# A causal mask, a key transpose and a sum of squares moved between TensorE and VectorE in a fused decoder layer

## The chip, the cores and the metric

The kernel runs on one core of one Trainium2 chip. The metric is the device time of one execution in microseconds; lower is better. The engines named below are TensorE (PE, matmuls and transposes through an identity), PEld (its weight loads), VectorE (DVE), ScalarE (ACT), GpSimd (POOL) and the DMA queues. PSUM is the memory that TensorE writes to, in banks of 128 partitions by 512 fp32 columns.

## The reference

One decoder layer over 256 tokens of width 2048, all fp32: a half-weighted SwiGLU block, a mixing layer, and another half-weighted SwiGLU block. The mixing layer has a sparse-attention branch and an mLSTM branch, each projected, gated and summed. What the change touches:

```python
def rms_norm(x, gain):
    x32 = x.astype(jnp.float32)
    y = x32 * lax.rsqrt(jnp.mean(x32 * x32, axis=-1, keepdims=True) + EPS)
    return (y * gain.astype(jnp.float32)).astype(x.dtype)

def masked_softmax(s, mask):
    s = jnp.where(mask, s.astype(jnp.float32), NEG_INF)
    return jax.nn.softmax(s, axis=-1) * mask
...
    # nsa_attention: 16 query heads in 4 groups, head width 64
    q = rms_norm(q, q_gain) * (d ** -0.5)
    p_cmp = masked_softmax(jnp.einsum("bgrsd,bgcd->bgrsc", q, kc), cmp_mask)
    kb = rms_norm(k_slc, ks_gain)      # keys of the selected blocks
    kw = rms_norm(k_win, kw_gain)      # keys of the window
    ps = masked_softmax(ss, smask)     # q against the selected keys, causal
    pw = masked_softmax(jnp.einsum("bgrqd,bgkd->bgrqk", qi, kwi), wmask)   # window, causal
    return gt[..., 0:1] * o_cmp + gt[..., 1:2] * o_slc + gt[..., 2:3] * o_win
```

With 256 tokens every block is selected and the window covers everything, so both the selected and the window attention are plain causal attention with keys and values of their own.

## The kernel before, in words

**Weights.** Every projection streams its weight from HBM in tiles of 128x1024 fp32 (512 KB). ScalarE rounds a tile to a high part (whi) and VectorE subtracts it to get a low part (wlo, split_lo); TensorE multiplies high and low parts with high and low parts of the activations, in matmuls of 512 or 256 columns that accumulate in the banks named mm. A unit is one block of output columns. Each tile is processed in two halves (e = 0 and 1) of six matmuls of 512 columns or their equivalent.

**Side work.** Everything else (norms, attention, mLSTM) is written as Python generators called jobs, which alternate: one part that issues TensorE work into a side bank (names sc and tr, two banks each), a yield, one part for the other engines, a yield. After each half tile, step() may let one job issue its TensorE part between the weight matmuls; uptake() issues the other part. All of this happens when the program is built: the order of the instructions on each engine is fixed, and Estimate keeps a running count of each engine's time from simple costs of shape and engine. A job is taken only under this rule in step(), with LAG = 4.0 and MARGIN = 0.3:

```python
if max(est.q["V"], est.q["A"]) > now + LAG or max(free["sc"][0], free["tr"][0]) > now:
    return None
j = next((j for j in jobs if ready(j) + MARGIN <= now and j is not cur.get("late")), None)
```

Jobs whose name begins with ca or R have their matmuls spread among the next weight matmuls, two or three at a time (mul). drain() issues all jobs that are left, one after another, with no weight matmuls between them.

**Norms.** residual() accumulates the squares of 16 blocks of the transposed activations in acc (128 x 2 x 256, even blocks in one half and odd ones in the other). The job g_r then sums over partitions with matmuls against a matrix of ones, which are fp32 and run in two passes each, computes 1/sqrt on VectorE and spreads it over a row (RB). It runs three times, as R0, R1 and R2.

**Attention.** normed() normalises queries and keys per head. g_kk(g) transposes the keys of group g, for both kinds of keys, and writes high and low parts (kk) into both partition halves. g_nsa() goes through 32 items: 4 groups, two halves t of the queries (the second has 256 keys, the first 128) and 4 heads. Step n transposes the probabilities of item n-3 and issues the scores of item n (both kinds of keys in one bank) and, as a third matmul, the mask: an identity in bf16 times the mask maskb, added in the bank. Then exps() takes the maximum on VectorE and exponentials on ScalarE, and scale() scales the item before on VectorE. After each four items pv() multiplies with the values. Between groups the job waits for g_ca (attention over compressed keys) and g_kk of the next group. After a step it yields the time at which the work of the item before last is done.

**Order around it.** The attention runs beside the units mv and mo of the mLSTM's projections. The next unit begins with mlstm_open(), which calls drain() before it can give the attention's memory to the mLSTM. In the profile this drain lies between 988.9 and 1007.8 us. g_mlstm has two mask matmuls per head of its own, which the change leaves alone.

Of the kernel before, what the change touches and what calls it, by code (L numbers as in the profile page):

```python
# [18 lines left out]
S = 256  # L19
# [95 lines left out]
def layer(ctx: ExitStack, tc: tile.TileContext, xt, cols, w_small, b_in,  # L115
# [282 lines left out]

    def g_r():

        ps = psS()
        for t in range(2):
            for a in range(2):
                T.matmul(ps[:, 2 * t:2 * t + 2], acc[:, a, t * 128:t * 128 + 128], ones[:, 0:2], start=a == 0, stop=a == 1)
        yield
        R = small(2, tag="R", bufs=2)
        rsqrt(R, ps[:, 0:4].rearrange("p (t e) -> p t e", e=2)[:, :, 0], 2, 1.0 / D)
        for t in range(2):
            V.tensor_scalar(dg[:, t, :], ident, R[:, t:t + 1], None, op0=OP.mult)
        cur["R"] = R  # L410
        yield
        ps = psS()
        for t in range(2):
            T.matmul(ps[:, t * 128:t * 128 + 128], ones, dg[:, t, :], start=True, stop=True)
        yield
        A.copy(RB, ps[:, :S])
        yield
# [134 lines left out]
    def mixing():  # L552
# [31 lines left out]
        def start():  # L584
            close1()
            openp("O")
            openp("V", "right")
            openp("N")
            O, N = env["O"], env["N"]
            env["O_"] = O.tile([128, 8, 2, S], F32R, name="O_")  # L590
            env["brow"] = O.tile([128, 384], F32R, name="brow")
            env["gat"] = O.tile([128, 2, 48], F32, name="gat")
            env["negM"] = O.tile([128, 2, 4], F32, name="negM")
            env["em"] = O.tile([128, 2, 4], F32, name="em")
            env["kn"] = N.tile([128, 2, 2, S], F32, name="kn")
            env["v"] = N.tile([128, 2, 2, S], F32, name="v")
            env["kc"] = N.tile([128, 4, 2, 32], F32R, name="kc")
            env["vcz"] = N.tile([128, 4, 4, 64], F32, name="vcz")
            nc.sync.dma_start(w2k, cw2k.rearrange("(k p) n -> p k n", p=128))
            nc.sync.dma_start(w2v, cw2v.rearrange("(k p) n -> p k n", p=128))  # L600
            G.memset(env["brow"].bitcast(F32), 0.0)
            G.memset(env["kc"].bitcast(F32), 0.0)
# [146 lines left out]
        def normed(src, dst, n):  # L749

            yield
            sq = t4() if n == 16 else t2()
            A.activation(sq, src, AF.Square)
            yield
            yield
            ss = small(n, tag="ss", bufs=2)
            V.tensor_reduce(ss, sq.rearrange("p t (h d) -> p (t h) d", d=64), AX, OP.add)
            yield
            yield
            rs = small(n, tag="rs", bufs=2)  # L760
            rsqrt(rs, ss, n, 1.0 / 64)
            yield
            yield
            V.tensor_mul(dst.rearrange("p t (h d) -> p (t h) d", d=64),
                         src.rearrange("p t (h d) -> p (t h) d", d=64),
                         rs[:, :, None].to_broadcast([128, n, 64]))
            yield

        def q_done(c):
# [13 lines left out]
            return f  # L783

        def g_qn(q, c):
            yield from normed(q, q, 16)
            if c == 0:
                env["qg"] = env["N"].tile([128, 1], F32, name="qg")
                V.tensor_scalar(env["qg"], col(C_QG), 0.125, None, op0=OP.mult)
# [19 lines left out]
        def g_kk(g):  # L809

            kk = env["k", g] = env["N"].tile([128, 2, 2, S], F32R, name=nm("kk"), tag="kk", bufs=2)
            tr = psT()[0:64].rearrange("p (i s) -> p i s", i=2)
            for i in range(2):
                for t in range(2):
                    T.transpose(tr[:, i, t * 128:t * 128 + 128], env["kn"][:, i, t, g * 64:g * 64 + 64], ident)
            yield
            each = [(i, cl[0:64, cg:cg + 1], slice(o, o + 64)) for i, cg in enumerate((C_KSG, C_KWG)) for o in (0, 64)]
            for i, gain, o in each:
                A.activation(kk[o, 0, i, :], tr[:, i, :], AF.Identity, scale=gain)
            for i, gain, o in each:  # L820
                V.scalar_tensor_tensor(kk[o, 1, i, :], tr[:, i, :], gain, kk[o, 0, i, :].bitcast(F32),
                                       op0=OP.mult, op1=OP.subtract)
            yield

# [6 lines left out]
            return f  # L831

        def g_k(k, i):
            yield from normed(k, env["kn"][:, i], 8)


        def gates_of(g):
# [37 lines left out]
        def g_nsa():  # L875
# [3 lines left out]
            def scores(g, t, r):  # L879
                n = 128 * (t + 1)  # L880
                ps = psS().rearrange("p (b s) -> p b s", b=2)
                for i in range(2):
                    T.matmul(ps[:, :, 0:n], env["q", g][:, r, t * 128:t * 128 + 128], env["k", g][:, i, :, 0:n],
                             start=i == 0, stop=False)
                T.matmul(ps[:, :, n - 128:n], identb, maskb[:, None, :].to_broadcast([128, 2, 128]),
                         start=False, stop=True)
                return ps

            def exps(g, t, r, ps):
                n = 128 * (t + 1)  # L890
                nx, sm = small(2, tag="nx", bufs=6), small(2, tag="nx", bufs=6)
                V.tensor_reduce(nx, ps[:, :, 0:n], AX, OP.max, negate=True)
                p = t2(n)
                for b in range(2):
# [524 lines left out]
```

## Time and profile before

| | |
|---|---|
| median of 3 runs | 2196.39 us (2196.3 to 2196.83) |
| the profiled execution | 2196.61 us |
| span of its instructions | 2194.9 us, 28308 instructions |
| TensorE busy | 2182.7 us (99%), 10865 matmuls |
| VectorE busy | 1429.3 us (65%) |
| ScalarE busy | 1043.8 us (48%) |
| DMA | 414 MB, 189 GB/s mean |

The span goes from the first to the last instruction in the profile; 1.7 us of the execution lie outside it. All instructions carry line 110, that of the helper which records each operation, so groups are told apart by engine, operation and tile names (out<-in). Tile names are cut to their letters: t is any of several scratch tiles, nx a maximum, sc and tr the side banks.

### The profile page before, as it was taken

Reading aid. Unit: us, or ns where it says so; the run is one execution under the profiler, and the core shown is the slowest. Engines: PE = TensorE matmul, PEld = TensorE weight load, DVE = VectorE, ACT = ScalarE, POOL = GpSimd, SP = SyncE. Lnnn points to the kernel's source line nnn. Section 1 sums busy time; section 2 is a strip of 40 time slices with the busy share of each in tenths; the row PEclk is TensorE's granted clock in tenths of the full one; section 3 lists DMA queues with packets and bytes.
Section 4 is the critical chain, followed back from the end, with each engine's and each line's share of the span. In section 5 each row is a group of like instructions: output and inputs, shape, how many; then the busy total and the mean of one; then the engine's idle time right before and its main releaser. Section 6 shows DMA issues by size and latency. Waiting matters only on the chain.

```text
span 2194.9 us, 28308 instructions
## 1 busy us (share of the span) xinstructions
PE 2182.7 (99%) x10865; PEld 1833.8 (84%) x10865; DVE 1429.3 (65%) x1895; ACT 1043.8 (48%) x1302; POOL 32.1 (1%) x62
## 2 busy tenths in 40 slices
PE   9999999999999999999999999999999999999999
PEld 7888888888888888777888888888888888888888
DVE  6766676666555678876777666666667666765554
ACT  6444444444444465666764444555444444443432
POOL 0000000000000000001100000000000000000000
PEclk9999999999999999999999999999999999999999
DMA  7666666666665676544556666566666666666664
GB/s 251 185 204 195 192 182 202 195 189 196 189 188 179 196 238 185 163 132 118 163 168 206 199 205 200 174 201 185 199 186 196 195 199 184 198 195 200 196 199 125
DMA packets 281047, 414.45 MB, mean 189 GB/s; under 512 B 13456, under 2 KB 146704, under 8 KB 280912
## 3 DMA queue, kind: packets, MB, share of 16 engines
q1 hardware_dynamic: 279408, 408.08, 61.2%
q0 software_dynamic: 1360, 4.46, 0.8%
q8 instruction: 85, 1.39, 0.3%
q14 instruction: 50, 0.41, 0.1%
q10 hardware_dynamic: 144, 0.11, 0.0%
HBM read 410.50 MB, written 2.10 MB: 188 GB/s over the span
## 4 chain that ended last, share of the span: by engine, by line
PE 97%; DVE 1%; DMA 0%; ACT 0%; issue 0%; SPq 0%; DVEq 0%; ACTq 0%
PE mm L110 94%; PE tr L110 2%; PE sc L110 2%; DVE wlo L110 0%; DMA raw<-in_wu_dram 0%; DMA raw<-in_w_in_dram 0%; DVE nx L110 0%; DVE t L110 0%; DVE y L110 0%; ACT t L110 0%; ACT whi L110 0%; ACT kk L110 0%; DVE mo L110 0%; DVE rt L110 0%; DVE kk L110 0%
## 5 line engine op out<-in xcount | busy, mean ns | idle before, releaser
L110 DVE TENSOR_TENSOR wlo<-raw,whi 128x1024 fp32r<-128x1024 f32 (+1 forms) x771 | 936.6, 1226 | 617.2 <-ACT whi L110 613.5
L110 PE MATMUL mm<-whi,XX 128*128 128x512 f32 x3904 | 1222.1, 391 | 4.9 <-ACT whi L110 4.9
L110 ACT CAST whi<-raw 128x1024 fp32r<-128x1024 f32 (+1 forms) x771 | 804.1, 1050 | 885.8 <-PE mm L110 843.5
L110 PEld LDWEIGHTS mm<-whi,XX 128*128 128x128 f32 x3904 | 734.3, 188 | 156.5 <-ACT whi L110 4.9
L110 PE MATMUL mm<-wlo,XX 128*128 128x512 f32 x1952 | 762.8, 391 | 0.5 <-DVE wlo L110 0.5
L110 PE MATMUL mm<-H,whi 128*128 128x512 f32 (+1 forms) x1496 | 446.4, 382 | 0.5 <-DVE y L110 0.5
L110 PEld LDWEIGHTS mm<-wlo,XX 128*128 128x128 f32 x1952 | 367.2, 188 | 75.6 <-DVE wlo L110 2.0
L110 PEld LDWEIGHTS mm<-H,wlo 128*128 128x128 f32 x1408 | 264.8, 188 | 58.6
L110 PE MATMUL mm<-H,wlo 128*128 128x256 f32 x1408 | 284.2, 278 | 0.0
L110 PEld LDWEIGHTS mm<-H,whi 128*128 128x128 f32 x1496 | 228.5, 189 | 0.9 <-DVE y L110 0.7
L110 DVE STREAM_TRANSPOSE ht<-sh 32x256 f32<-32x256 f32 x352 | 153.5, 436 | 6.4
L110 PE MATMUL mm<-XX,whi 128*128 128x512 f32 x272 | 87.7, 401 | 0.0
L110 PE MATMUL mm<-M__9899,whi 128*128 128x512 f32 x256 | 80.0, 394 | 0.0
L110 PEld LDWEIGHTS mm<-XX,wlo 128*128 128x128 f32 x272 | 51.0, 188 | 12.0 <-DVE wlo L110 0.7
L110 PEld LDWEIGHTS mm<-M__9899,wlo 128*128 128x128 f32 x256 | 48.1, 188 | 10.9
L110 PE MATMUL mm<-XX,wlo 128*128 128x256 f32 x272 | 55.0, 279 | 0.2 <-DVE wlo L110 0.2
L110 PE MATMUL mm<-M__9899,wlo 128*128 128x256 f32 x256 | 50.5, 279 | 0.0
L110 PEld LDWEIGHTS mm<-XX,whi 128*128 128x128 f32 x272 | 42.3, 189 | 1.0 <-issue 0.2
L110 ACT ACTIVATE sg<-mm,R 128x512 f32<-128x512 f32 x40 | 25.4, 686 | 33.0 <-PE mm L110 31.6
L110 PE MATMUL mm<-whi,h__8408 128*128 128x512 f32 x128 | 40.2, 390 | 0.0
L110 PE MATMUL mm<-whi,O__5735 128*128 128x512 f32 x128 | 40.1, 389 | 0.0
L110 PEld LDWEIGHTS mm<-M__9899,whi 128*128 128x128 f32 x256 | 38.6, 188 | 0.1
(192 smaller groups left out, 969.0 us busy)
## 6 DMA issues: line engine op xcount, KB each, us to landing
raw<-in_wu_dram SPq DMA_DIRECT2D x176, 512.0 KB, 3.9
raw<-in_wd_dram SPq DMA_DIRECT2D x176, 512.0 KB, 4.7
raw<-in_wg_dram SPq DMA_DIRECT2D x175, 512.0 KB, 4.4
raw<-in_w_in_dram SPq DMA_DIRECT2D x168, 512.0 KB, 3.8
raw<-in_w_out_dram SPq DMA_DIRECT2D x32, 512.0 KB, 4.7
raw<-in_wb_n_dram SPq DMA_DIRECT2D x16, 512.0 KB, 4.7
raw<-in_wb_m_dram SPq DMA_DIRECT2D x16, 512.0 KB, 4.0
bias<-in_b_in_dram POOLq DMA_DIRECT2D x17, 256.0 KB, 4.0
```

The source lines that it names most:

```text
L110: return g(out, *a, **k)
```

## The change

Three edits. The mask matmul of the attention's scores is gone; instead VectorE adds the mask to the last 128 columns of both halves of the bank, in place, before it takes the maximum. The normalised keys are stored with the two kinds side by side for each group (kn becomes token half, group, kind, width), so that one transpose of 128 columns holds both kinds, one kind in each partition half, and g_kk issues two transposes, not four. In g_r VectorE first adds the two halves of acc, in a step of its own, and the sum over partitions takes two matmuls, not four.

```diff
     def g_r():
 
+        yield
+        V.tensor_add(acc[:, 0], acc[:, 0], acc[:, 1])
+        yield
         ps = psS()
         for t in range(2):
-            for a in range(2):
-                T.matmul(ps[:, 2 * t:2 * t + 2], acc[:, a, t * 128:t * 128 + 128], ones[:, 0:2], start=a == 0, stop=a == 1)
+            T.matmul(ps[:, 2 * t:2 * t + 2], acc[:, 0, t * 128:t * 128 + 128], ones[:, 0:2], start=True, stop=True)
...
-            env["kn"] = N.tile([128, 2, 2, S], F32, name="kn")
+            env["kn"] = N.tile([128, 2, 4, 2, 64], F32, name="kn")
...
-            V.tensor_mul(dst.rearrange("p t (h d) -> p (t h) d", d=64),
-                         src.rearrange("p t (h d) -> p (t h) d", d=64),
-                         rs[:, :, None].to_broadcast([128, n, 64]))
+            V.tensor_mul(dst, src.rearrange("p t (h d) -> p t h d", d=64),
+                         rs.rearrange("p (t h) -> p t h", t=2)[:, :, :, None].to_broadcast([128, 2, n // 2, 64]))
...
-            yield from normed(q, q, 16)
+            yield from normed(q, q.rearrange("p t (h d) -> p t h d", d=64), 16)
...
-            tr = psT()[0:64].rearrange("p (i s) -> p i s", i=2)
-            for i in range(2):
-                for t in range(2):
-                    T.transpose(tr[:, i, t * 128:t * 128 + 128], env["kn"][:, i, t, g * 64:g * 64 + 64], ident)
+            tr = psT()[:, 0:S]
+            for t in range(2):
+                T.transpose(tr[:, t * 128:t * 128 + 128], env["kn"][:, t, g].rearrange("p i d -> p (i d)"), ident)
             yield
-            each = [(i, cl[0:64, cg:cg + 1], slice(o, o + 64)) for i, cg in enumerate((C_KSG, C_KWG)) for o in (0, 64)]
-            for i, gain, o in each:
-                A.activation(kk[o, 0, i, :], tr[:, i, :], AF.Identity, scale=gain)
-            for i, gain, o in each:
-                V.scalar_tensor_tensor(kk[o, 1, i, :], tr[:, i, :], gain, kk[o, 0, i, :].bitcast(F32),
+            each = [(i, slice(64 * i, 64 * i + 64), cg, slice(o, o + 64)) for i, cg in enumerate((C_KSG, C_KWG)) for o in (0, 64)]
+            for i, s, cg, o in each:
+                A.activation(kk[o, 0, i, :], tr[s], AF.Identity, scale=cl[s, cg:cg + 1])
+            for i, s, cg, o in each:
+                V.scalar_tensor_tensor(kk[o, 1, i, :], tr[s], cl[s, cg:cg + 1], kk[o, 0, i, :].bitcast(F32),
                                        op0=OP.mult, op1=OP.subtract)
...
-            yield from normed(k, env["kn"][:, i], 8)
+            yield from normed(k, env["kn"][:, :, :, i, :], 8)
...
                     T.matmul(ps[:, :, 0:n], env["q", g][:, r, t * 128:t * 128 + 128], env["k", g][:, i, :, 0:n],
-                             start=i == 0, stop=False)
-                T.matmul(ps[:, :, n - 128:n], identb, maskb[:, None, :].to_broadcast([128, 2, 128]),
-                         start=False, stop=True)
+                             start=i == 0, stop=i == 1)
                 return ps
...
                 nx, sm = small(2, tag="nx", bufs=6), small(2, tag="nx", bufs=6)
+                own = ps[:, :, n - 128:n]
+                V.tensor_add(own, own, maskb[:, None, :].to_broadcast([128, 2, 128]))
                 V.tensor_reduce(nx, ps[:, :, 0:n], AX, OP.max, negate=True)
```

## Rows read from the trace of the kernel before

**Rows 1.** The profile's page: busy time of each engine with its share of the span and its instructions, and the chain that ended last, by engine.

```profile
PE 2182.7 (99%) x10865; PEld 1833.8 (84%) x10865; DVE 1429.3 (65%) x1895; ACT 1043.8 (48%) x1302; POOL 32.1 (1%) x62
...
PE 97%; DVE 1%; DMA 0%; ACT 0%; issue 0%; SPq 0%; DVEq 0%; ACTq 0%
```

**Rows 2.** Groups of matmuls by shape over the whole span: the costliest one and the three that the change edits. The columns are the shape, how many, busy us and mean ns of one, and the idle time before them.

```profile
L110 PE MATMUL mm<-whi,XX 128*128 128x512 f32 x3904 | 1222.1, 391 | 4.9 <-ACT whi L110 4.9
...
L110 PE MATMUL sc<-maskb,identb 128*128 128x256 bf16 x32 | 9.1, 283 | 0.0
...
L110 PE MATMUL sc<-ones,acc 128*128 128x2 f32 x24 | 3.0, 230 | 0.0
...
L110 PE MATMUL tr<-ident,kn 128*64 128x128 f32 x16 | 2.4, 272 | 0.0
```

**Rows 3.** The timeline of TensorE in five short stretches: start, length from the first start to the modelled last end, and how many matmuls of one kind. Left-out lines inside a stretch are weight matmuls (mm, 512 columns), one unless said: one at 848.09; one at 882.14; one at 889.38; one at 49.82 and two from 50.50; in the last stretch, which is one item, two transposes of 128 columns at 904.85, two scores of 512 at 904.99, the mask at 905.54 and one weight matmul at 905.58.

```profile
48.99 0.62 PE L110 MATMUL mm<-whi,XX 128*128 128x512 f32 x2
49.45 0.50 PE L110 MATMUL sc<-ones,acc 128*128 128x2 f32 x4
...
50.13 0.50 PE L110 MATMUL sc<-ones,acc 128*128 128x2 f32 x4
...
51.04 0.40 PE L110 MATMUL mm<-wlo,XX 128*128 128x512 f32 x1
...
847.50 0.40 PE L110 MATMUL mm<-whi,XX 128*128 128x512 f32 x1
847.73 0.60 PE L110 MATMUL tr<-ident,kn 128*64 128x128 f32 x4
...
848.40 0.39 PE L110 MATMUL mm<-wlo,XX 128*128 128x512 f32 x1
...
881.54 0.63 PE L110 MATMUL mm<-whi,XX 128*128 128x512 f32 x2
882.00 0.38 PE L110 MATMUL tr<-ident,t 128*128 128x128 f32 x2
...
882.45 0.63 PE L110 MATMUL mm<-whi,XX 128*128 128x512 f32 x2
...
888.86 0.40 PE L110 MATMUL mm<-whi,XX 128*128 128x512 f32 x1
889.09 0.40 PE L110 MATMUL sc<-kk,qs 128*128 128x256 f32 x2
889.34 0.28 PE L110 MATMUL sc<-maskb,identb 128*128 128x256 bf16 x1
...
889.69 0.39 PE L110 MATMUL mm<-wlo,XX 128*128 128x512 f32 x1
...
904.61 0.40 PE L110 MATMUL mm<-whi,XX 128*128 128x512 f32 x1
...
905.90 0.39 PE L110 MATMUL mm<-wlo,XX 128*128 128x512 f32 x1
```

**Rows 4.** Windows: the stretch in us and its length, then busy time (and instructions) of PE, PEld, DVE, ACT and POOL, the granted TensorE clock (1.00 is full), the DMA share and GB/s. First the 25 us before the attention, all of the attention among weight matmuls, and the drain; then three stretches in which items of 256 keys run, and as the second of the four one with items of 128 keys.

```profile
864.00:889.00 25.00, 24.24 (x120) 19.88 (x119) 22.55 (x45) 14.53 (x18) 0.54 (x1) 1.00 0.65 190
889.00:988.90 99.90, 99.90 (x561) 77.78 (x559) 79.19 (x163) 61.99 (x170) 1.08 (x2) 1.00 0.49 142
988.90:1007.80 18.90, 17.15 (x127) 11.76 (x125) 13.09 (x40) 13.17 (x53) 0.00 (x0) 1.00 0.11 29
...
898.10:910.90 12.80, 12.80 (x66) 9.79 (x66) 11.26 (x24) 9.54 (x30) 0.00 (x0) 1.00 0.57 165
917.50:932.30 14.80, 14.80 (x96) 11.80 (x95) 11.88 (x26) 8.24 (x27) 0.54 (x1) 1.00 0.56 162
932.30:945.70 13.40, 13.40 (x68) 10.26 (x67) 11.56 (x28) 8.36 (x24) 0.00 (x0) 1.00 0.44 127
...
969.20:985.00 15.80, 15.80 (x82) 12.40 (x81) 12.38 (x27) 8.98 (x23) 0.00 (x0) 1.00 0.40 106
```

**Rows 5.** The timeline of VectorE in the drain, where items of 256 keys run; the bracket at the end of a line is idle time before it and what ended it.

```profile
996.37 0.42 DVE L110 TENSOR_TENSOR O__5735<-tr,O__5735 128x256 fp32r<-128x256 f32 x1 [1.37 <-ACT O__5735 L110]
...
998.22 0.68 DVE L110 TENSOR_REDUCE nx<-sc 128x2 f32<-128x512 f32 x1
998.82 0.15 DVE L110 RECIPROCAL nx<-nx 128x2 f32<-128x2 f32 x1
999.01 0.73 DVE L110 TENSOR_SCALAR t<-t,nx,gat 128x256 f32<-128x256 f32 x2
999.67 0.69 DVE L110 TENSOR_REDUCE nx<-sc 128x2 f32<-128x512 f32 x1
...
1001.12 0.68 DVE L110 TENSOR_REDUCE nx<-sc 128x2 f32<-128x512 f32 x1
```

**Rows 6.** Groups of VectorE instructions by shape over the whole span, columns as in the second group of rows: the queries' low parts, an mLSTM product with three operands, and the add of the compressed scores' mask.

```profile
L110 DVE SCALAR_TENSOR_TENSOR qs<-tr,qg,qs 64x512 fp32r<-64x512 f32 x8 | 6.0, 750 | 4.9 <-ACT qs L110 4.8
...
L110 DVE SCALAR_TENSOR_TENSOR h<-tr,rc,mo 128x256 f32<-128x256 f32 x8 | 3.5, 480 | 0.1
...
L110 DVE TENSOR_TENSOR t<-sc,mcb 128x256 f32<-128x256 f32 x4 | 1.7, 423 | 2.1 <-PE sc L110 2.1
```

**Rows 7.** The instructions on the tile R, the norm's factors: the gates that are scaled by it from PSUM (how many, duration least, median and most in ns, then first and last start in us).

```profile
L110 ACT ACTIVATE sg<-mm,R x40: 682/686/691, 79.6 to 1923.2; 128x512 f32<-128x512 f32 x40
```

**Rows 8.** Who waited for whom, all of the span: TensorE's weight matmuls for the low parts of weights (us in total, times, longest).

```profile
PE mm L110 <- DVE wlo L110: 0.7, 3, 0.3
```

## The prediction

> **What bounds the kernel now.** I read the totals first, then single shapes, then stages. In the totals [rows 1] TensorE is busy 99% of the span and the chain that ended last runs over it for 97%; VectorE is at 65%. Shape by shape [rows 2] nearly all of that is the streamed weights, matmuls of 512 columns; the reader is to see how small the edited shapes are beside them. Their starts [rows 3] lie 0.23 us apart when one follows another: that pitch, not the 0.39 us that a single one lasts, is what a removed matmul is worth. So a TensorE instruction taken out between weight matmuls shortens the run by its pitch.
>
> That holds only where weights stream. The windows by stage [rows 4] show two other places. In the 99.9 us of attention VectorE is already busy 79.2 us, and in the best-filled stretches about 88% of the time. And from 988.9 to 1007.8 the kernel drains: the last unit of VectorE-fed projections is over, mlstm_open calls drain(), and no weight matmul stands between the attention steps. All eight items of the last group lie there. VectorE's rows in the drain [rows 5] are the ones to look at longest: its maxima of the second half begin at 998.22, 999.67 and 1001.12, 1.45 us apart, and the four VectorE pieces in each stretch (maximum, reciprocal, two scalings) follow each other without a gap. There VectorE sets the pace. TensorE's busy row claims 17.15 of 18.9 us for this drain, its weight loads only 11.76.
>
> [...] By the matmul row TensorE would bound the drain, its 0.12 us per mask would count there in full, and the adds would be worth minus 1.0 instead of the plus 2.7 below; by the weight-load row the drain is VectorE's. The gapless 1.45 us decide for the second.
>
> **The parts, on TensorE.** Mask: between the weight matmuls that begin at 888.86 and 889.69 lie two plain pitches (0.46) and three matmuls of 256 columns, two scores and a mask [rows 3]: 0.83 - 0.46 = 0.37, so 0.12 us a mask. There are 32 in attention (the eight of 128 columns belong to the mLSTM and stay) [rows 2]: 3.8 us, of which 24 among weights now, 2.9.
>
> Keys: four transposes of 64 columns cost 847.50 to 848.40 less two pitches, 0.44; two of 128 columns cost 881.54 to 882.45 less three pitches, 0.22 [rows 3]. Four groups, 0.88 us.
>
> Squares: each of three norms issues two runs of four (two fp32 passes per matmul) [rows 2, 3]. From 48.99 to 51.04 are five pitches (1.15) and both runs: 0.90, one run 0.45. With two matmuls kept, not four, one run is left: 3 x 0.45 = 1.35 us.
>
> **On VectorE.** 32 adds of 128x256 with one operand in PSUM. The nearest row is the same add for the compressed scores, also with a bf16 mask, 423 ns [rows 6]; that one writes to SBUF, and no row has VectorE writing to PSUM. Lower bound 0.33, the pitch of two such scalings when nothing depends on the first [rows 5]; upper 0.48, a three-operand pass over 256 elements [rows 6]. I take 0.42, as the shape is the same: 13.4 us in all. The three adds of halves (two operands of 128x256 again, so 0.42) are hidden: the norm's factors have many half tiles before a unit's end wants them (the first sums run at 49.45, the first gate is scaled from PSUM at 79.6 [rows 3, 7]), and the additional step costs about one half tile, 1.4 us. Should that cover be gone it costs 3 x 1.8. The other layout of kn changes strides only, same shapes and counts; gains on partitions 64 to 127 into 0 to 63 are what qs does already (750 ns for twice the columns) [rows 6]. Nothing here issues a DMA or moves one past a queue: the weight tiles keep their places.
>
> The add waits for the score as the maximum did. Behind it on VectorE stand the maximum, the scaling of the item before and the next weight split (wlo). The exponential waits for the first, the transposes for the second, weight matmuls for the third. That wait is short now: 0.7 us in all [rows 8].
>
> **Drain as it stands.** Eight adds. The fourth falls into the 1.37 us that VectorE idles before 996.37 [rows 5]; seven are on the pace: 7 x 0.42 = 2.9, less 0.2 for scores that come earlier without a mask at the two places where VectorE has just waited: plus 2.7. Bounds: 7 x 0.33 less eight masks (1.0), plus 1.3; 8 x 0.48, plus 3.8.
>
> **What slips into it.** This is where I chose. In the stretches in which items of 256 keys run, VectorE is busy 11.26 of 12.8, 11.56 of 13.4 and 12.38 of 15.8 us [rows 4]. Each gets four adds, 1.7 us, and loses four masks, 0.5 us of TensorE: 12.96 in 12.3, 13.26 in 12.9, 14.1 in 15.3. The first two are over-full. The planner in the code doesn't let VectorE fall far behind: no job when its count for VectorE is over 4.0 ahead, nor before the banks of the item before last are free. So it skips half tiles, and the splits go on taking VectorE. If 0.89 is the best fill (11.26/12.8, 22.55/25 [rows 4]), the three need 14.6, 14.9 and 15.8 us, 2.3 + 2.0 + 0.5 more; the half-group of 128 keys at 917.5 (11.88 + 1.7 = 13.6, by 0.89 15.3, against 14.3) 1.0 more. That is 5.8 us, four half tiles of 1.4. A group alternates items with other steps, so about three items are not issued in time, and the compressed attention of the last group, which ends just before the drain now, has its last two steps in it as well.
>
> An item in the drain costs VectorE 1.45 + 0.42 = 1.87. The work that TensorE takes along is worth 904.61 to 905.90 less two pitches and a mask [rows 3]: 1.29 - 0.46 - 0.12 = 0.71. Net 1.16; three, 3.5 us. The compressed steps: a sum, two products of 256 elements at 0.33 and some small ones, 1.35, with the wait for the exponential about 1.7.
>
> **Sum.** 21 masks among weights -2.5, keys -0.88, squares -1.35, drain +2.7, three items +3.5, compressed steps +1.7: +3.2 us. On the profiled execution (2196.61: span 2194.9 and 1.7 around it) that is 2199.8; the median of the runs is 0.2 lower, so 2199.6.
>
> **The rivals.** (1) Nothing slips: VectorE has 20.7 idle us in attention against 24 x 0.42 = 10.1. For it: the total fits, and the third stretch has room. Against: the idle time lies around the p-v steps and group changes, where no item may start. Then -2.9 - 0.88 - 1.35 + 2.7 = -2.4: 2194.0, with the drain's bounds 2192.6 to 2195.1.
> (2) Five to seven items slip and the compressed attention comes late whole (2.5): -2.2 - 0.88 - 1.35 + 2.7 + 5.8 to 8.1 + 2.5, plus 6.6 to 8.9: 2203.0 to 2205.3. It decides when the first group loses three half tiles or more, since the later ones start from its backlog. For it: VectorE at 22.55 of 25 us before attention begins; against: the p-v steps in which it catches up.
> (3) The change is worth all it removes: the new order leaves no more exposed in the drain than today's, 3.8 + 0.88 + 1.35 = 6.0: 2190.4. The gapless pieces of the drain speak against it.
> (4) TensorE's clock falls in the longer, sparser drain. [...]
>
> **How the numbers follow.** Forecast (two to four items slip, 2198.2 to 2201.2 with the bounds of the add) 0.54; (1) 0.18; (2) 0.19; (3) 0.05; (4) 0.04. The range 2193.0 to 2204.5 leaves out (3), the low end of (1) and the top of (2). A measurement here tells 0.2%, 4.4 us, from no change: 2192.0 and 2200.8. Faster: (3) and a little of (1), 0.07. Slower: (2), (4) and the upper part of the forecast, 0.38. Same: 0.55.
>
> **What would show it.** In the profile after: no maskb matmul in attention; eight kn transposes, twelve ones matmuls; a VectorE add on sc near 0.42 us, 32 times; VectorE over 85% in attention; more than eight score pairs in the drain, with maxima near 1.9 us apart; a drain some 8 us longer and an attention stage shorter. Wrong if the drain still begins with the last group, if it begins deeper than four items before it, if weight matmuls wait for wlo, or if the clock leaves 1.00.

## The result, and the profile after

| | before | after |
|---|---|---|
| median of 4 runs side by side | 2196.46 us (2196.3 to 2196.83) | 2212.9 us (2212.35 to 2213.21) |
| ratio, 95% interval | | 1.0075, 1.0063 to 1.0088 |
| the profiled execution and its span | 2196.61, 2194.9 us | 2212.35, 2210.0 us |

The change costs 16.4 us. That is slower by more than the 0.2% a measurement here can tell, and 8.4 us above the upper end of the range.

First the totals of the profile after, then the groups that the change edits.

```profile
span 2210.0 us, 28239 instructions
PE 2184.4 (99%) x10813; PEld 1835.5 (83%) x10813; DVE 1443.7 (65%) x1930; ACT 1045.3 (47%) x1302; POOL 32.0 (1%) x62
...
L110 DVE TENSOR_TENSOR sc<-sc,maskb 128x256 f32<-128x256 f32 x32 | 13.7, 427 | 2.6 <-PE sc L110 2.6
L110 DVE TENSOR_TENSOR acc<-acc 128x256 f32<-128x256 f32 x3 | 1.3, 419 | 0.0
...
L110 PE MATMUL tr<-ident,kn 128*128 128x128 f32 x8 | 1.5, 272 | 0.0
L110 PE MATMUL sc<-ones,acc 128*128 128x2 f32 x12 | 1.5, 230 | 0.0
```

Each edit did what it says: against [rows 2] the 32 masks are gone from TensorE, and the transposes of kn and the matmuls against ones have halved in number. The in-place add in PSUM takes 427 ns, the forecast's 0.42. And yet the totals hardly tell that 15 us were lost: TensorE's busy row is at 99% as in [rows 1]. The windows by stage tell it. Columns as in [rows 4]; of before, cut at the last weight matmul ahead of the drain (which [rows 4] cuts 1.6 us later):

```profile
889.00:987.30 98.30, 98.30 (x544) 76.77 (x542) 77.84 (x161) 61.76 (x170) 1.08 (x2) 1.00 0.49 142
987.30:1007.80 20.50, 18.75 (x142) 12.77 (x141) 14.43 (x41) 13.39 (x54) 0.00 (x0) 1.00 0.13 36
```

The same windows of after, cut in the same way, and two short ones from its drain:

```profile
888.40:971.90 83.50, 83.50 (x425) 67.83 (x423) 68.44 (x129) 49.99 (x122) 1.07 (x2) 1.00 0.53 157
971.90:1023.40 51.50, 36.95 (x224) 25.00 (x223) 37.58 (x105) 26.43 (x102) 0.00 (x0) 0.80 0.11 31
...
980.00:984.00 4.00, 3.51 (x16) 2.35 (x18) 3.48 (x12) 3.21 (x15) 0.00 (x0) 0.50 0.00 0
996.00:1000.00 4.00, 1.54 (x8) 0.86 (x10) 2.19 (x7) 1.39 (x5) 0.00 (x0) 0.50 0.00 0
```

The attention among weight matmuls became 14.8 us shorter, and the drain 31 us longer, 51.5 for 20.5. Two things are new. VectorE fills only 68.44 of the stage's 83.5 us, 82%: the stage isn't over-full, steps were left out of it. And the granted clock, 1.00 in every window shown of before, is 0.80 over the drain and 0.50 in parts of it, the two short windows among them.

The timeline of TensorE in the drain after; the bracket is idle time and what ended it.

```profile
971.72 0.39 PE L110 MATMUL mm<-whi,XX 128*128 128x512 f32 x1
972.03 1.08 PE L110 MATMUL tr<-pt,v 128*64 128x256 f32 x8
...
974.57 0.63 PE L110 MATMUL tr<-ident,t 128*128 128x128 f32 x4 [1.02 <-DVE kk L110]
974.95 0.48 PE L110 MATMUL sc<-kk,qs 128*128 128x256 f32 x2
...
978.83 0.76 PE L110 MATMUL tr<-ident,t 128*128 128x128 f32 x4 [2.00 <-DVE t L110]
...
981.57 3.68 PE L110 MATMUL tr<-pt,v 128*64 128x256 f32 x16
985.04 1.07 PE L110 MATMUL tr<-pc,vcz 128*64 128x128 f32 x8
...
989.49 1.60 PE L110 MATMUL sc<-kc,qs 128*128 128x64 f32 x8 [1.46 <-ACT t L110]
...
998.46 0.66 PE L110 MATMUL tr<-ident,t 128*128 128x128 f32 x2 [4.26 <-DVE t L110]
...
1014.77 0.74 PE L110 MATMUL sc<-kk,qs 128*128 128x512 f32 x2
```

971.72 is the last weight matmul. Of the pairs of scores (sc<-kk) that follow, the first and the last stand here and fourteen lie between them: sixteen items, all of the last two groups, where before had eight. The last compressed attention lies in the drain as well, whole (sc<-kc at 989.49), and TensorE waits 4.26 us for VectorE to finish it. The 16 p-v matmuls (probabilities times values, tr<-pt,v) at 981.57 take 3.47 us until the next start; before, the same 16 took 1.78 (993.53 to 995.31).

VectorE in the same place, while TensorE waits:

```profile
993.30 0.69 DVE L110 TENSOR_REDUCE nx<-sc 128x2 f32<-128x512 f32 x1
993.91 0.16 DVE L110 RECIPROCAL nx<-nx 128x2 f32<-128x2 f32 x1
994.10 0.74 DVE L110 TENSOR_SCALAR t<-t,nx,gat 128x256 f32<-128x256 f32 x2
994.75 0.43 DVE L110 TENSOR_TENSOR sc<-sc,maskb 128x256 f32<-128x256 f32 x1
995.22 0.69 DVE L110 TENSOR_REDUCE nx<-sc 128x2 f32<-128x512 f32 x1
```

From maximum to maximum it is 1.92 us without a gap, where [rows 5] had 1.45 and the forecast 1.87.

Who waited for whom, on TensorE over the whole span (us in total, times, longest); the wait for a weight split had 0.7 us before [rows 8], and the first line was 0.3 in the attention before.

```profile
PE tr L110 <- DVE t L110: 9.7, 7, 4.3
...
PE mm L110 <- DVE wlo L110: 1.4, 3, 0.8
```

### The profile page after: what moved, and what is told of

The parts are those of the page before. It is cut to its first block, busy times and chain, and to the rows that moved or that the text cites. A ratio compares the mean times of both kernels' runs of the same rounds, so it can differ in the third digit from the quotient of the medians.

```text
span 2210.0 us, 28239 instructions
## 1 busy us (share of the span) xinstructions
PE 2184.4 (99%) x10813; PEld 1835.5 (83%) x10813; DVE 1443.7 (65%) x1930; ACT 1045.3 (47%) x1302; POOL 32.0 (1%) x62
## 3 DMA queue, kind: packets, MB, share of 16 engines
q8 instruction: 84, 1.38, 0.3%
## 4 chain that ended last, share of the span: by engine, by line
PE 96%; DVE 2%; DMA 0%; ACT 0%; issue 0%; SPq 0%; DVEq 0%; ACTq 0%
PE mm L110 93%; PE tr L110 2%; PE sc L110 1%; DVE wlo L110 0%; DVE t L110 0%; DVE nx L110 0%; DMA raw<-in_wu_dram 0%; DMA raw<-in_w_in_dram 0%; DVE sc L110 0%; DVE y L110 0%; DVE kk L110 0%; ACT t L110 0%; ACT qs L110 0%; ACT whi L110 0%; ACT kk L110 0%
## 5 line engine op out<-in xcount | busy, mean ns | idle before, releaser
L110 ACT ACTIVATE t<-sc,nx 128x128 f32<-128x128 f32 (+1 forms) x64 | 26.4, 418 | 36.3 <-DVE nx L110 36.3
```

What stands on the lines that cost most here:

```text
L110: return g(out, *a, **k)
```

## The experiments

Two theories stood at the start. **Order**: the planner in the code counts each add (0.13 us + 256/960, so 0.40 us, in Estimate), refuses half tiles by its own count, and pushes items into the drain; the time goes there. **Work**: the add itself, on a VectorE that is nearly full, delays what follows, whatever the order is. Later the clock came up as a third. The kernel before ran at 2196.0 to 2196.5 us beside each of them. The table has them all; "drain" is from the last weight matmul to the next one, with the items in it, by the profiles. Those of a1 and b2 are of their slowest executions (2195.66 and 2207.27 us).

| | median (range, runs), us | ratio, 95% interval | drain, us | items |
|---|---|---|---|---|
| a1_keys_squares | 2194.63 (2193.62 to 2195.66, 11) | 0.9992, 0.9983 to 1.0001 | 20.6 | 8 |
| a2_mask | 2212.77 (2212.64 to 2214.38, 4) | 1.0077, 1.0063 to 1.0091 | 51.9 | 16 |
| b1_uncounted | 2203.02 (2201.24 to 2204.69, 6) | 1.0031, 1.0019 to 1.0042 | 28.8 | 9 |
| b2_counted_only | 2204.71 (2204.41 to 2207.27, 4) | 1.0041, 1.0027 to 1.0055 | 44.6 | 16 |
| b3_same_order | 2200.9 (2198.75 to 2203.57, 11) | 1.0022, 1.0014 to 1.0031 | 26.8 | 8 |
| d5_same_order_last_mm | 2196.67 (2195.95 to 2198.61, 11) | 1.0002, 0.9993 to 1.0011 | 22.5 | 8 |
| c_lag5 | 2206.91 (2206.11 to 2208.52, 4) | 1.0051, 1.0037 to 1.0064 | 42.5 | 13 |
| e_warm2 | 2212.82 (2211.69 to 2214.66, 4) | 1.0077, 1.0064 to 1.0091 | 52.0 | 16 |
| g1_b3_warm | 2198.92 (2197.66 to 2199.91, 11) | 1.0012, 1.0003 to 1.0021 | 25.0 | 8 |
| g2_after_warm | 2209.44 (2208.03 to 2209.55, 4) | 1.006, 1.0043 to 1.0076 | 49.7 | 16 |
| f1_some_adds | 2193.44 (2192.89 to 2193.96, 11) | 0.9989, 0.998 to 0.9998 | 21.3 | 8 |

### The parts one by one

**a1_keys_squares** is the change without its mask edit:

```diff
-                             start=i == 0, stop=i == 1)
+                             start=i == 0, stop=False)
+                T.matmul(ps[:, :, n - 128:n], identb, maskb[:, None, :].to_broadcast([128, 2, 128]),
+                         start=False, stop=True)
...
-                own = ps[:, :, n - 128:n]
-                V.tensor_add(own, own, maskb[:, None, :].to_broadcast([128, 2, 128]))
```

> The keys' and the squares' edits alone; the mask stays a matmul. Every theory has this small: by the pitches read from the kernel before, four times 0.22 and three times 0.45 us less TensorE, 2.2 us faster than before (2194.2), with 8 of the 32 score pairs in the drain as before. If one of these two edits were what lengthens the drain, the time would be 2205 or more and more than 8 score pairs would lie in the drain.

**a2_mask** is the opposite: the kernel before with the mask edit alone.

> The mask's edit alone; keys and squares as before. If the mask's add is the cause, whether by the planner's order or by VectorE itself: 2213 to 2217, that is after and the 2.2 us of the other two edits, with 16 score pairs in the drain. If the cause is an interplay of the three edits: under 2205.

Measured: 2194.63 and 2212.77, the second 0.2 under its range. The mask edit alone carries all of the loss. Keys and squares are worth 1.5 us against the 2.2 of the sum, with an interval of the ratio that holds both (minus 3.7 to plus 0.2 us).

### Order or work

Four kernels hold one of the two still. **b1_uncounted** does the adds but hides them from the planner:

```diff
-                V.tensor_add(own, own, maskb[:, None, :].to_broadcast([128, 2, 128]))
+                nc.vector.tensor_add(own, own, maskb[:, None, :].to_broadcast([128, 2, 128]))
```

> The change complete, but the planner's running count for VectorE leaves the mask's add out, so the order stays nearly that of before: 9 score pairs in the drain, not 16. VectorE does the same 32 adds. Theory order (the planner's count moves items into the drain, and what is exposed there is the loss): 2194 to 2198, that is 2196.5 less 2.9 for masks, 0.9 for keys and 1.35 for squares, plus 2.7 to 3.8 for the adds in the drain and 1 to 2.5 for the one item and the last step of the compressed attention that slip. Theory engine (VectorE can't do the adds beside the weight splits, whatever the order): 2206 or more, with TensorE waiting among weight matmuls for wlo or for the probabilities, several us in all.

**b2_counted_only** lets the planner count adds that aren't there; the mask is the old matmul, uncounted, so that the order is that of the change:

```diff
-                             start=i == 0, stop=i == 1)
+                             start=i == 0, stop=False)
+                nc.tensor.matmul(ps[:, :, n - 128:n], identb, maskb[:, None, :].to_broadcast([128, 2, 128]),
+                         start=False, stop=True)
...
-                V.tensor_add(own, own, maskb[:, None, :].to_broadcast([128, 2, 128]))
+                est.spend("V", est.cost("V", "tensor_add", own, (), {}))
```

> The counterpart: the planner counts the mask's add on VectorE and no matmul for it, so the order is that of after, but the add is not done; the mask is a matmul as before. Theory order: the drain begins as deep as after, with 16 score pairs in it, and the time stays far above before: 2206 to 2211, that is 2212.9 less about 0.42 for each of the 16 items whose add is on VectorE's pace there (6.7) and plus 2 for the 16 masks among weights. Theory engine: without the adds the time falls back to before, 2194 to 2198.

Measured: 2203.02 and 2204.71. Each theory alone explains only a part of the loss: with the adds hidden from the planner some 7 of the 16.4 us stay, and with the adds absent but counted some 9. Both expectations were missed: b1 lies between the ranges of the two theories, b2 1.3 us under the one for order. What the order alone does is seen in the timeline of b2's drain:

```profile
995.98 0.66 PE L110 MATMUL tr<-ident,t 128*128 128x128 f32 x2 [4.32 <-DVE t L110]
```

These are the transposes that wait 4.26 us in the kernel after. No add is done in b2, and the wait is as long: it comes with the order.

b1 still has nine items in its drain, as TensorE's missing mask also moves the planner's count. So **b3_same_order** also keeps that count, and the order is that of a1:

```diff
                     T.matmul(ps[:, :, 0:n], env["q", g][:, r, t * 128:t * 128 + 128], env["k", g][:, i, :, 0:n],
                              start=i == 0, stop=i == 1)
+                est.spend("T", 256 / 2400.0 + 0.0025)
...
-                V.tensor_add(own, own, maskb[:, None, :].to_broadcast([128, 2, 128]))
+                nc.vector.tensor_add(own, own, maskb[:, None, :].to_broadcast([128, 2, 128]))
```

> The change complete, with the planner's count as if the mask were still a matmul: the order of every instruction is that of a1_keys_squares, only 32 adds on VectorE stand where 32 mask matmuls stood. 8 score pairs in the drain. Theory order alone: 2194.4, that is 2194.6 less 2.9 for 24 masks among weights and plus 2.7 for the adds in the drain (2193 to 2196). Theory engine as well (a VectorE this full starts the drain with work left over and lets TensorE wait in the attention stage too): 2198 to 2203, most of what b1_uncounted lost.

Measured: 2200.9, in the range for both theories. With a1, b2 and the kernel after this makes a square of four:

| | mask by TensorE | mask by VectorE | the work |
|---|---|---|---|
| a1's order | 2194.6 (a1) | 2200.9 (b3) | +6.3 |
| the change's order | 2204.7 (b2) | 2212.9 (after) | +8.2 |
| the order | +10.1 | +12.0 | |

Both theories hold, order being the larger by the medians. Each of the four differences is uncertain by 3 to 4 us by the intervals in the table, so the two rows, and the two columns, don't differ clearly from each other. Where the work costs time in an unchanged order is seen in the windows of b3, its stage and its drain:

```profile
888.60:985.90 97.30, 95.64 (x515) 76.05 (x514) 86.50 (x181) 59.29 (x165) 1.07 (x2) 1.00 0.46 137
985.90:1012.80 26.90, 20.57 (x135) 13.60 (x133) 18.71 (x53) 15.33 (x58) 0.00 (x0) 0.87 0.18 52
```

The window of a1's stage:

```profile
889.00:986.80 97.80, 97.80 (x540) 76.47 (x538) 78.10 (x161) 61.56 (x170) 1.07 (x2) 1.00 0.48 142
```

VectorE's share of the stage is 89% for 80%, and TensorE, which never waited in a1's stage, is no longer busy throughout. **d5_same_order_last_mm** separates stage and drain: b3, but the last group, which lies in the drain, keeps its mask matmul.

```diff
-                             start=i == 0, stop=i == 1)
-                est.spend("T", 256 / 2400.0 + 0.0025)
+                             start=i == 0, stop=i == 1 and g < 3)
+                if g < 3:
+                    est.spend("T", 256 / 2400.0 + 0.0025)
+                else:
+                    T.matmul(ps[:, :, n - 128:n], identb, maskb[:, None, :].to_broadcast([128, 2, 128]),
+                             start=False, stop=True)
...
-                own = ps[:, :, n - 128:n]
-                nc.vector.tensor_add(own, own, maskb[:, None, :].to_broadcast([128, 2, 128]))
+                if g < 3:
+                    own = ps[:, :, n - 128:n]
+                    nc.vector.tensor_add(own, own, maskb[:, None, :].to_broadcast([128, 2, 128]))
```

> As b3_same_order, but the masks of the last group, whose 8 items lie in the drain, stay matmuls; the 24 others are adds that the planner doesn't count. If the adds cost only in the drain: 2191.7 (2190.5 to 2193), 2.9 less than a1_keys_squares. If the adds in the attention stage cost too: 2194 to 2199.

Measured: 2196.67, in the range for adds that cost in the stage too: it is 2.0 above a1, although 24 masks of 0.12 us, 2.9 us by [rows 3], have left the weight matmuls. So by the medians the 24 adds cost 2.0 + 2.9 = 4.9 us in waits, and the last group's eight adds 4.2 more (b3 less d5). Three windows at the end of the first group show where the first waits lie. Those of a1:

```profile
905.00:910.00 5.00, 5.00 (x30) 3.84 (x28) 4.43 (x11) 3.70 (x14) 0.00 (x0) 1.00 0.50 160
910.00:914.00 4.00, 4.00 (x20) 3.27 (x19) 2.44 (x3) 3.91 (x8) 0.00 (x0) 1.00 0.44 131
914.00:918.00 4.00, 4.00 (x31) 2.83 (x30) 3.16 (x5) 2.18 (x5) 0.00 (x0) 1.00 0.00 0
```

The same windows of d5:

```profile
905.00:910.00 5.00, 4.80 (x24) 3.35 (x22) 4.86 (x12) 3.24 (x11) 0.00 (x0) 1.00 0.66 203
910.00:914.00 4.00, 3.19 (x14) 2.35 (x14) 3.06 (x5) 3.94 (x10) 0.00 (x0) 1.00 0.26 71
914.00:918.00 4.00, 3.30 (x24) 2.41 (x25) 2.42 (x6) 3.04 (x6) 0.00 (x0) 1.00 0.16 60
```

VectorE is busy 4.86 of 5 us in d5's first window; the price comes in the next two, where the steps between groups need what VectorE is late with. The timeline of d5 names two of them, and the third, at the start of its drain:

```profile
910.51 0.44 PE L110 MATMUL tr<-ident,kn 128*128 128x128 f32 x2 [0.61 <-ACT pt L110]
...
914.33 1.08 PE L110 MATMUL tr<-pt,v 128*64 128x256 f32 x8 [0.63 <-DVE qs L110]
...
991.48 0.76 PE L110 MATMUL tr<-ident,t 128*128 128x128 f32 x4 [1.87 <-DVE t L110]
```

a1 waits at none of the three. The scores of the second group's first item begin at 917.65 us in a1 and at 918.19 in d5, though d5 had been 1.4 us ahead one item earlier (907.40 and 905.98): 2.0 us are lost there. 1.9 more are the wait at 991.48, VectorE's backlog at the drain's start. These two places hold 3.9 us; between the profiled executions of a1 and d5 (2195.66 and 2196.57 us) the adds cost 0.9 + 2.9 = 3.8.

**c_lag5** varies the dose of the order: the change, with the planner's leave for VectorE and ScalarE raised from 4.0 to 5.0.

```diff
-LAG = 4.0
+LAG = 5.0
```

> The change complete and counted, with the planner's limit for VectorE's lead raised from 4.0 to 5.0: by the built order 12 score pairs lie in the drain, not 16. Theory order: between 8 items (2194.6) and 16 items (2212.9), by a straight line 2203.8; 2201 to 2206. If not the number of items in the drain but VectorE's work decides: 2210 to 2214.

Measured: 2206.91, 0.9 above the range, with 13 items in the drain and not 12. The last compressed attention lies in it whole, as in the kernel after. From 8 items (b3) to 13 and the compressed attention it is 6.0 us, from 13 to 16 (after) another 6.0. So the price of an item isn't constant. A part of this is the clock, whose mean over the drain is 0.87 in b3, 0.88 in c_lag5 and 0.80 in after. As an estimate from these means, that is about 7, 10 and 21 us at 0.50, the lowest in any window read.

### The clock

**g1_b3_warm** is b3 with matmuls of 512 columns that nobody reads, in two places of its drain: eight in the longest wait, after the second item's scores, and three after the third's:

```diff
+                if j[2] == "nsa":
+                    seen[0] += 1
+                    for _ in range({3: 8, 4: 3}.get(seen[0], 0)):
...
+                        nc.tensor.matmul(warm[0][:, 0, :].rearrange("p (a b) -> p a b", b=128), identb,
+                                         maskb[:, None, :].to_broadcast([128, 4, 128]), start=True, stop=True)
```

In the drain of b3 (2200.9 us) the granted clock is 0.71 from 990 to 994 us, 0.50 from 994 to 996, 0.62 from 996 to 999.3 and 1.00 around them; by these means it is an estimated 6.8 us at 0.50. Its 16 p-v products run from 995.16 to the next start at 998.56.

> [...] If the lower clock costs time: the clock stays at 1.00, the same products take 1.8 to 2.4 us, and the time is 2199.0 to 2199.8. If it is hidden: 2200.4 to 2201.4 with the clock at 1.00. If the clock falls all the same, nothing is learned.

The window around the waits, of b3:

```profile
990.00:994.00 4.00, 1.54 (x6) 1.21 (x6) 3.86 (x13) 1.77 (x9) 0.00 (x0) 0.71 0.44 131
```

The timeline of TensorE there, of b3:

```profile
992.41 1.11 PE L110 MATMUL tr<-ident,t 128*128 128x128 f32 x4 [2.46 <-DVE t L110]
...
995.16 3.57 PE L110 MATMUL tr<-pt,v 128*64 128x256 f32 x16
998.56 0.60 PE L110 MATMUL tr<-pc,vcz 128*64 128x128 f32 x8
```

The same window of g1:

```profile
990.00:994.00 4.00, 3.26 (x18) 1.50 (x16) 3.86 (x13) 2.06 (x11) 0.00 (x0) 1.00 0.46 131
```

The same place in the timeline of g1:

```profile
994.68 1.95 PE L110 MATMUL tr<-pt,v 128*64 128x256 f32 x16
996.46 0.61 PE L110 MATMUL tr<-pc,vcz 128*64 128x128 f32 x8
```

TensorE was busy 1.54 of the 4 us in which b3's clock fell; with 3.26 us in the same window of g1 the profiled drain keeps 1.00 throughout, VectorE's 3.86 unchanged, and the p-v run takes 1.78 us until the next start instead of 3.40. Measured: 2198.92, 2.0 below b3, and 0.1 under the range for a clock that costs time. So the clock is about 2.0 of b3's 6.3 us; the executions of the two overlap, but the p-v run alone is 1.6 us shorter in the traces. Executions of one kernel say the same with no edit between them: in d5 six had a mean clock of 1.000 and took 2195.95 to 2196.67 us, five had 0.999 and took 2196.8 to 2198.61. Five of g1's eleven were at 0.999 as well, so 2.0 is rather too little than too much.

**e_warm2** and **g2_after_warm** ask the same of the kernel after. e_warm2 puts two such matmuls behind every step of the drain; g2 puts 8, 2, 1, 5 and 16 into five places of it, four of them waits.

In the kernel after (2212.9 us) the first run of 24 p-v products takes 4.47 us to the next transposes (981.57 to 986.04), for 2.32 before (993.53 to 995.85, at 1.00). The second, of 16, takes 2.76 (999.05 to 1001.81), for 1.45 of a like run in g1 at 1.00 (985.91 to 987.36).

> The change complete, with two matmuls of 512 columns (bf16, no reader) after each TensorE step of the drain, to keep the granted clock up; else after's order. If the lower clock in the drain costs time: the clock stays above 0.9 in all of the drain and 2207 to 2211, that is 4 to 5 us less for p-v products at full speed and 0 to 2 us for the added matmuls. If the lower clock is hidden under waits: 2212 to 2216.

> The change complete and counted, order of after, with 32 matmuls of 512 columns that nothing reads put only where after's drain lets TensorE wait longest (8 after the third-group's second item, 2 and 1 after the next two, 5 and 16 before and in the wait for the last compressed attention). [...] If the lower clock costs: 2208.5 to 2210.5 with the clock at 1.00 in most of the drain. If hidden: 2212 to 2214. e_warm2 came out at 2212.8 with the clock up, but its added matmuls stood in the p-v products' way as well.

Measured: 2212.82 and 2209.44. e_warm2 raised the mean clock of the profiled execution from 0.995 to 0.999 and gained nothing, so it lies in the range given for a clock that is hidden. But it tells nothing apart: where TensorE had no wait, each of its pairs puts off the attention's next step by 0.44 us (from 983.18 to 983.62, for one), and the last six the next weight matmul by 1.1. g2, in the range for a clock that costs, brought 3.5 us at a mean clock of 0.998. Its clock still fell twice in the profiled drain (1.00 from 972 to 990 us, 0.89 from 990 to 1020), once at the very end, where that of after is at 1.00 and its last 15 p-v matmuls take 1.78 us until the next start, for 3.12 in g2. So 3.5 us or more of the loss are the clock's.

### A version that beats both

**f1_some_adds** is a1 (its order and its matmuls) with adds only for the 14 items from the first of the second group on, where the first group's waits are past and the backlog can be worked off before the drain:

```diff
-                             start=i == 0, stop=False)
-                T.matmul(ps[:, :, n - 128:n], identb, maskb[:, None, :].to_broadcast([128, 2, 128]),
-                         start=False, stop=True)
+                             start=i == 0, stop=i == 1 and (g in (1, 2) and (g, t, r) < (2, 1, 2)))
+                if g in (1, 2) and (g, t, r) < (2, 1, 2):
+                    est.spend("T", 256 / 2400.0 + 0.0025)
+                else:
+                    T.matmul(ps[:, :, n - 128:n], identb, maskb[:, None, :].to_broadcast([128, 2, 128]),
+                             start=False, stop=True)
...
+                if g in (1, 2) and (g, t, r) < (2, 1, 2):
+                    own = ps[:, :, n - 128:n]
+                    nc.vector.tensor_add(own, own, maskb[:, None, :].to_broadcast([128, 2, 128]))
```

> Keys and squares as in the change; the mask is an add only for 14 items of the second and third groups (not the third's last two), not counted by the planner, and a matmul for the first group, where d5_same_order_last_mm lost 2 us of waits, and in the drain. The order is that of a1_keys_squares. If VectorE has room there: 2194.6 less 14 times 0.12, 2192.9 (2192.3 to 2193.8), and no clear wait of TensorE in the attention stage. If any add costs as much as the average of d5's 24 (4.9 us of waits): 2195 to 2196.

The window of its stage, columns as in [rows 4]:

```profile
887.00:983.00 96.00, 96.00 (x526) 76.20 (x524) 83.57 (x175) 60.51 (x171) 1.08 (x2) 1.00 0.47 142
```

VectorE is at 87% and TensorE never waits. Measured: 2193.44, in the range for adds that find room, a ratio to before of 0.9989 (0.998 to 0.9998), 19.5 us under the kernel after. Against a1 it is 1.2 us; 14 masks of 0.12 are 1.7. The two have no interval of their own, and their runs overlap slightly.

## Why the prediction was wrong

The forecast was plus 3.2 us; it is plus 16.4. By the runs this is made up of minus 1.5 (keys and squares), plus 6.3 (VectorE's work in an unchanged order) and plus 12.0 (the order with the work in it), within half a microsecond. Taken the other way round the square, it is plus 10.1 for the order and plus 8.2 for the work.

**Right: the drain's terms, and their prices in total.** The add: 0.427 for 0.42. The pace in the drain: 1.92 for 1.87. That the drain is VectorE's, not TensorE's, which the choice between TensorE's matmul row and its weight-load row decided: b3 less d5 is a cost, 4.2 us, or 2.2 without the clock (g1) where the sum had 2.7; by the matmul row eight adds would have been a gain. The price of a slipped item, 1.16, and of the whole compressed attention, 2.5: eight items and it make 11.8 us, and the order costs 12.0. At least 1.5 of these (3.5 by g2 less 2.0 by g1) are the clock's. That the total fits so well is partly luck, as c_lag5 shows: by these prices its five items and the compressed attention cost 8.3 and the last three items 3.5, and both were 6.0.

**Wrong: how many items slip.** This is the step that failed, "If 0.89 is the best fill (...) about three items". Eight slipped, and the compressed attention whole. With this number the forecast's own prices give plus 10.3, so the step accounts for 7 of the missing 13 us. The mechanism was the forecast's: the planner's count for VectorE pushes the items out (nine in the drain where it leaves the adds out, b1; sixteen where it counts adds that aren't there, b2). Rival (2) was closer, at five to seven items, and not deep enough.

The count went wrong in the working. The sum over the stretches leaves out the first four items, and they lie in a fuller stretch than any that it counts. The window of before, columns as in [rows 4]:

```profile
889.00:898.10 9.10, 9.10 (x48) 7.50 (x47) 8.52 (x18) 4.25 (x15) 0.54 (x1) 1.00 0.64 195
```

This is a fill of 0.94, so 0.89 wasn't the best one. By the prediction's rule these four items need 10.2 / 0.89 = 11.5 us (8.52 and four adds) where 8.6 are left: 2.9 us more, 8.7 for 5.8 in all. That is six half tiles and not four, by its conversion four or five items.

The result also hangs strongly on the fill. Worked from the windows after, as an estimate: 83.5 us with 16 items hold 68.44 of VectorE. An item more brings about 1.5 us to TensorE (the last weight matmul ahead of the drain begins 15.4 us earlier, 2 to 4 of it by masks, keys and squares, the rest by eight items) and 2.46 to VectorE (77.84 less 68.44 plus 16 adds, by 8, and an add). At a fill of 0.89 that gives 5 items more, a slip of three, as forecast. The planner reached 0.82, a slip of eight. Nothing slips only at about 0.92, and at 0.79, the fill of the whole stage before (79.2 of 99.9 [rows 4]), ten do. This sensitivity was in no range. A fill read from a trace can't settle the number: it is fixed by the planner's counts when the program is built, as b2 shows.

**Wrong: a term left out.** This and the clock are the other 6 of the missing 13 us. The work of the adds in an unchanged order stood in the sum at minus 2.9 for the masks that leave the stage and plus 2.7 for the drain; that a fuller VectorE makes TensorE wait in the steps between groups, and starts the drain with a backlog, wasn't in it. d5 puts this at 4.9 us. The prediction named the waiting queue (maximum, scaling, weight split) but judged it by the 0.7 us of [rows 8], which is the wait of weight matmuls. That one stayed small, 1.4 us, none of it in the attention; it was the attention's own steps that waited, for pt, qs and t. Rival (1), in which nothing slips, wasn't 2194.0 therefore: b3 is its experiment, and it took 2200.9. Only with the adds put where there is room, in f1, does a time near it come out, with 14 adds, not 32. In the kernel after the term shows in another place: its stage has no wait at all (83.50 of 83.50 us busy), but its drain begins with VectorE behind (waits of 1.02 and 2.00 us at 974.57 and 978.83, where b2, without adds, has none and 1.38).

**Wrong: the clock.** Rival (4), given 0.04, took place together with the slip. No row of before showed how far the clock would fall or what that would cost: it was 1.00 in every window. The runs show 0.80 over the drain of after, 0.50 in parts of it, and 3.5 us or more, which lie within the terms above. The prediction treated it as another way to go. In the runs it came with the longer waits: b3, in which no item slips, has lost it already. Its drain is at 0.87, with TensorE busy 1.54 us between 990 and 994; that of d5, with 2.45 us there, is at 1.00; and in g1 the drain of b3 is at 1.00, by matmuls that nobody reads.

**What the forecast's own signs say.** Over 85% of VectorE in the attention: no, 82%, and this was the telling one. More than eight pairs in the drain, at 1.9 us: yes, sixteen. A drain 8 us longer: 31. Of the four signs that would make it wrong, two came, a drain deeper than four items and a clock that left 1.00.

**Still open.** The backlog at the drain's start and the waits between groups are told apart in d5 by their places, not by runs of their own. Whether the keys and squares reach their 2.2 us can't be told from their 1.5. How a slipped item's price divides between VectorE's pace and the clock isn't shown either.

## What to carry to other kernels

Where a program plans its order by its own cost counts, an operation moved to an engine costs twice: the work itself, and what the planner then refuses to issue; a square of four kernels (counted or not, done or not) tells the two apart, each run beside the same kernel. Count what slips from the planner itself, since the order is fixed when the program is built; where a fill read from a trace stands in for it, take all stretches and vary the fill before believing the count. Moving work from the bound engine to one at 80% paid here only where that engine had room: 14 of 32 masks, the order kept, gained about a microsecond (1.2, within the scatter of the runs); all 32 lost 6.3 in the same order and more than sixteen as the planner placed them.

## What the runs showed of the hardware that was not expected

TensorE's granted clock fell to 0.50 within a drain that lasts 27 us in b3 (0.71 from 990 to 994 us, 0.50 in the next 2 us): in a 4 us stretch in which TensorE was busy 1.54 us and which holds most of a single wait of 2.46 us for VectorE; the profiled drains of a1, d5 and f1 kept 1.00. While it was down, the same 16 p-v matmuls took 3.40 to 3.47 us for 1.78. Eleven unread matmuls of 512 columns in two places kept it at 1.00 in the profiled execution and paid 2.0 us, with no other edit. VectorE's add in place in PSUM with a broadcast bf16 operand takes 427 ns for 128x256, as its PSUM-to-SBUF form does (423 [rows 6]).
